# Head norms, attention and gating of a decoder trunk handed out in smaller, later pieces

## The chip, the cores and the metric

The kernel runs on one core of a Trainium2 chip. The core has a matrix engine (TensorE, PE in the profile, with its weight loads shown as PEld), a vector engine (VectorE, DVE), an engine for functions of one input (ScalarE, ACT), a general one (GpSimd, POOL) and SyncE (SP), whose queue issues most DMAs. Each engine takes the instructions of its queue in order; between engines, semaphores hold an instruction back until its inputs are written and its output's buffer is free. The metric is the device time of one execution in microseconds (us); lower is better.

## The reference

Two layers over 256 tokens of width 2048, all in float32:

```python
for l in range(DEPTH):
    h = rms_norm(x, norm1_g[l])
    z = h @ w_in[l]                                  # u | v | q | k | v of attention
    z_sgu = jax.nn.gelu(z[..., :2 * SGU_WIDTH], approximate=False)
    out_a = chunked_sgu(z_sgu, sgu_norm_g[l], sgu_w[l], sgu_b[l])
    out_b = swa_sink_attention(z[..., 2*SGU_WIDTH:q_end], z[..., q_end:k_end], z[..., k_end:], ...)
    mixed = concat([rms_norm(out_a, out_norm_a[l]), rms_norm(out_b, out_norm_b[l])])
    x = x + mixed @ w_out[l]
    h2 = rms_norm(x, norm2_g[l])
    x = x + (jax.nn.silu(h2 @ w_gate[l]) * (h2 @ w_up[l])) @ w_down[l]
```

`chunked_sgu` normalizes v per head of 64 channels, mixes it over the 128 tokens of a chunk with a lower triangular matrix, adds a bias, and multiplies u by the result. `swa_sink_attention` normalizes q and k per head, takes scores over the own block of 128 keys and the one before, adds a relative bias with a mask, and applies a softmax that has one extra "sink" logit per head; 16 query heads share 4 key heads. The feed-forward width is 5632.

## The kernel before

**Main work.** Every weight matrix is read from HBM in blocks of 256 rows by 512 columns (`raw`, 128 partitions x 1024 elements). A weight block is split into a rounded part `wh` (ScalarE, L94) and the remainder `wl` (VectorE, L95), and the activations are held as such a pair too; a product is three matmuls, high by high, high by low and low by high (L124, L125, L126). The function `unit` does this for one block and the 256 tokens: 12 matmuls of 128x128 by 512 columns. It ends with `tick()`, which moves a clock of the program by 1. There are 7 buffers for `raw`, 5 for `wh` and 4 for `wl`, so ScalarE and VectorE can work some units ahead of TensorE.

**Layer.** The projection `w_in` is taken in column blocks of 512, eight units each (`in_block`): first k and v of attention (block 6), then q (4 and 5), then v of the gating part (2 and 3), then u (0 and 1). Then follow 32 units of the output projection in eight parts (`add_part`), and the feed-forward stage, which mixes two streams of units and whose code does not change but for one short step at its start.

**Short work between.** Everything else is placed by hand between the units: `later(delay, fn)` notes a function with the program's clock plus a delay, and `tick` calls, in the order of their time and then of their noting, those that are due. A fractional time is due at the next tick that reaches it. This gives the order in which the program is written. The framework's scheduler then makes each engine's queue from it, and assigns buffers.

- `kv_norm`, `q_norm` and `v_gate` take a finished block from PSUM with ScalarE (L259, L282, L413), and norm it per head by `head_inv`: squares on ScalarE (L207), sums on VectorE (L208), then in `inv_rms` mean and epsilon on VectorE (`ms`, L169) and the power -0.5 on GpSimd (`ir`, L171). VectorE then scales by the result (L265, L287, L417, and the gain L418). All that is written in one go, right after the block. Transposes for q and k follow 4 or 5 units later.
- `attend` does one of six pieces of attention in a layer, 6, 9, 12, 15, 19 and 23 units after the first q block (`UNIT_AT`). TensorE makes the scores (`ps_s`, L319), VectorE adds the bias (`s`, L324) and takes the maximum (L333) and from it `nm` and `es` (L334, L335), ScalarE takes the exponentials with their sums (L338) and that of the sink (L342), and VectorE makes the reciprocal `rden` (L343, L344). All that is written in one go. `turn`, two units later, transposes the probabilities (`ps_p`, L352) and copies them (`pt`, L353); `weigh`, four units later, multiplies by the values (`ps_v`, L361) and scales into `ob` (L368). `attend_end` comes 6 and 7 units after the third and the sixth piece: it sums squares of `ob` (L195), transposes it (`ps_t`, L188) and splits it into the pair `aT` (L178, L179).
- `v_gate` also loads the mixing matrix `wm` and the gain `gb` from GpSimd's queue (L388, L394), masks `wm` there (L389), and 6 and 7 units later runs the mixing matmuls (`ps_g`, L404) with the bias (L410).
- `u_gated` applies Gelu (L429), multiplies by the gate (L430) and sums squares, and 2 and 3 units later transposes.
- `finish_rms` sums partial squares (L199) and calls `inv_rms` for a norm over a row; `begin` does that for the first norm of a layer, and `nr` (L530 to L532) negates the second norm's result.

**Buffers.** Small PSUM tiles come in turn from four places (`small_ps`: one of pool `pm`, two of `pd`, one of the accumulators' pool `pa`). SBUF tiles with the tag `z` share 8 places, `big` 8, `spt` 4 (scores `s` and probabilities `pt`).

Of the kernel before, what the change touches and what calls it, by code (L numbers as in the profile page):

```python
# [12 lines left out]
F32 = mybir.dt.float32  # L13
F32R = mybir.dt.float32r
BF16 = mybir.dt.bfloat16
AF = mybir.ActivationFunctionType
# [4 lines left out]
P = 128  # L21
# [42 lines left out]
def trunk(ctx, tc, x, xt, w_in, w_out, w_gate, w_up, w_down, sgu_w, sgu_g, consts,  # L64
# [135 lines left out]
        r = inv_rms(tot, NTOK, width)  # L200
        return [r[:, t : t + 1] for t in range(NTOK)]

    def head_inv(zs, n):
        ss = small([P, NTOK * n], f"hs{n}")
        for t, z in enumerate(zs):
            sq = zp.tile([P, NB], F32, tag="z", name="sq")
            nc.scalar.activation(sq[:, : n * HD], z, AF.Square)  # L207
            nc.vector.tensor_reduce(  # L208
                ss[:, t * n : (t + 1) * n],
                sq[:, : n * HD].rearrange("p (h d) -> p h d", d=HD), AX.X, ALU.add,  # L210
            )
# [28 lines left out]
    for lay in range(L):  # L240
# [14 lines left out]
        def kv_norm(acc, lay=lay, layer=layer, zkv=zkv, kT=kT):  # L255
            kd = []
            zz = ap.tile([P, NTOK, NB], F32, tag="big", name="zkv", bufs=8)
            for t in range(NTOK):
                nc.scalar.activation(zz[:, t], acc[t], AF.Copy, scale=layer["rstd1"][t])  # L259
                zkv.append(zz[:, t])  # L260
            inv = head_inv([z[:, : NKV * HD] for z in zkv], NKV)
            for t in range(NTOK):
                k = zp.tile([P, NKV, HD], F32, tag="z", name="k")
                kin = zkv[t][:, : NKV * HD].rearrange("p (h d) -> p h d", d=HD)
                nc.vector.tensor_tensor(k, kin, bc(inv[t], HD), ALU.mult)  # L265
                kd.append(k.rearrange("p h d -> p (h d)"))
# [11 lines left out]
        def q_norm(b, acc, lay=lay, layer=layer, qT=qT):  # L278
            qn = []
            for t in range(NTOK):  # L280
                z = zp.tile([P, NB], F32, tag="z", name="zq")
                nc.scalar.activation(z, acc[t], AF.Copy, scale=layer["rstd1"][t])  # L282
                qn.append(z)
            inv = head_inv(qn, 8)
            for t in range(NTOK):
                z3 = qn[t].rearrange("p (h d) -> p h d", d=HD)
                nc.vector.tensor_tensor(z3, z3, bc(inv[t], HD), ALU.mult)  # L287
# [21 lines left out]
        def attend(gp, t, i0, n, zkv=zkv, kT=kT, qT=qT, ob=ob, bias=bias, layer=layer):  # L309
# [23 lines left out]
            nc.vector.tensor_reduce(m, s, AX.X, ALU.max)  # L333
            nc.vector.scalar_tensor_tensor(nm, m, -1.0, nsink, ALU.mult, ALU.min)  # L334
            nc.vector.tensor_tensor(es, nm, nsink, ALU.subtract)  # L335
            for r in range(2):
                for i in range(n):
                    nc.scalar.activation(  # L338
                        s[:, r, i], s[:, r, i], AF.Exp, bias=nm[:, r, i : i + 1],
                        accum_out=den[:, r, i : i + 1],  # L340
                    )
            nc.scalar.activation(es, es, AF.Exp)  # L342
            nc.vector.tensor_tensor(rden, den, es, ALU.add)  # L343
            nc.vector.reciprocal(rden, rden)  # L344
            pt = ap.tile([P, 8, P], F32, tag="spt", name="pt", bufs=4)
            s8 = s.rearrange("p r i (b k) -> p (r i b) k", k=P)

            def turn():
                for half in range(2):
                    pst = small_ps([P, 4, P], "ps_p")  # L350
                    for i in range(4):
                        nc.tensor.transpose(pst[:, i, :], s8[:, 4 * half + i, :], ident)  # L352
# [32 lines left out]
        def v_gate(b, acc, lay=lay, layer=layer, gate=gate):  # L385
# [28 lines left out]
            inv = head_inv([v[:, t] for t in range(NTOK)], 8)  # L414
            for t in range(NTOK):
                v3 = v[:, t].rearrange("p (h d) -> p h d", d=HD)
                nc.vector.tensor_tensor(v3, v3, bc(inv[t], HD), ALU.mult)  # L417
                nc.vector.tensor_tensor(v[:, t], v[:, t], gb, ALU.mult)  # L418
            for half in range(2):
                later(6 + half, lambda half=half: spatial(half))  # L420

# [3 lines left out]
        def u_gated(b, acc, lay=lay, layer=layer, gate=gate, ssa=ssa, pairs_a=pairs_a):  # L425
            us = []
            for t in range(NTOK):
                u = zp.tile([P, NB], F32, tag="z", name="u")
                nc.scalar.activation(u, acc[t], AF.Gelu, scale=layer["rstd1"][t])  # L429
                nc.vector.tensor_tensor(u, u, gate[b][:, t], ALU.mult)  # L430
                sum_sq(ssa[:, t, b : b + 1], u)
                us.append(u)

            def to_T(c):
                ps = transpose_pair([us[t][:, 2 * c * P : (2 * c + 2) * P] for t in range(NTOK)])
# [31 lines left out]
        def norm_block(n, ss, pairs, lay, col, ext=None):  # L467
# [11 lines left out]
            for t in range(NTOK):  # L479
                sum_sq(ss[:, t, n : n + 1], xres[:, t, n * NB : (n + 1) * NB])  # L480

        acc_kv = in_block(6)
        if lay == 0:
            later(5, begin)
            later(5, lambda: kv_norm(acc_kv))
        else:
            begin()
            kv_norm(acc_kv)
        acc = in_block(4)
        for g in range(2):  # L490
            load_bias(g)
# [24 lines left out]
        def add_part(n, pairs, chunks, rstd):  # L516
            acc = product([w_out[lay, n, c] for c in chunks], pairs)
            for t in range(NTOK):
                xs = xres[:, t, n * NB : (n + 1) * NB]
                nc.vector.scalar_tensor_tensor(xs, acc[t], rstd[t], xs, ALU.mult, ALU.add)  # L520

        for part, n in (("b", 0), ("b", 1), ("a", 0), ("a", 1), ("b", 2), ("a", 2), ("b", 3), ("a", 3)):
            if part == "b":
                add_part(n, pairs_b, range(4, 8), rstd_b)
            else:
                add_part(n, pairs_a, range(4), rstd_a)
# [4 lines left out]
        for t in range(NTOK):  # L531
            nc.vector.tensor_scalar(nr[:, t : t + 1], rstd2[t], -1.0, None, ALU.mult)  # L532
        nrstd2 = [nr[:, t : t + 1] for t in range(NTOK)]

        ss1 = small([P, NTOK, ND], "ss4")
        pairs1 = []
# [317 lines left out]
```

## Time and profile before

| | us |
|---|---|
| three runs: median (lowest, highest) | 1946.79 (1945.83, 1951.07) |
| the profiled execution: its time | 1945.39 |
| its span, first to last instruction | 1943.6 |
| TensorE busy | 1927.1 |
| VectorE busy | 1659.8 |
| ScalarE busy | 1301.4 |
| GpSimd busy | 122.0 |

The granted clock of TensorE was 1.00 throughout. A row of the page or of a view names an engine, a line of the kernel, an operation, what it writes and reads, and the shapes; then busy time and, in brackets, the idle time of the engine just before and what ended it. "PE ps_p L352 <- ACT s L338" reads: TensorE, about to write `ps_p` in line 352, waited for ScalarE writing `s` in line 338. Rows of a timeline start with the time and the duration in us. Busy spans of matmuls are modelled and overlap, so two consecutive ones count for less than their sum. Layer 0 reaches the feed-forward stage at about 300 us, layer 1 begins at about 975 us and reaches its own at about 1265 us.

### The profile page before, as it was taken

To read this page: it belongs to the slowest core of one execution; us is meant where nothing else is said; L and a number is where in the kernel's file an instruction comes from. 1 tells how busy PE (TensorE), PEld (TensorE's weight loads), DVE (VectorE), ACT (ScalarE), POOL (GpSimd) and SP (SyncE) were. 2 spreads that over 40 slices of the span, in tenths; PEclk is the share of its full clock that TensorE was granted. 3 is DMA by queue.
4 is the path that set the end of the run, shared out by engine and by line. 5 is a ranking of instruction groups with operands and counts; after the bars stand their busy time and mean duration, and the time that the engine had idled before them with its cause. 6 is when DMAs were issued, how large, how long until landed. Compare 5 with 4: busy or idle time off the path is not lost.

```text
span 1943.6 us, 25049 instructions
## 1 busy us (share of the span) xinstructions
PE 1927.1 (99%) x8836; PEld 1576.2 (81%) x8836; DVE 1659.8 (85%) x1752; ACT 1301.4 (67%) x1729; POOL 122.0 (6%) x124
## 2 busy tenths in 40 slices
PE   9999999999999999999999999999999999999999
PEld 6788887878888888888887888878788888888887
DVE  6566689999999999999556656899999999999993
ACT  7565566667767776777756755666677767767675
POOL 1210000000000000000002000000000000000000
PEclk9999999999999999999999999999999999999999
DMA  9544557667867786778555345586678676776783
GB/s 364 194 144 154 186 174 230 219 230 242 260 216 236 241 275 210 240 228 271 195 198 191 132 164 183 169 260 213 212 241 280 211 242 225 269 218 236 238 264 125
DMA packets 118958, 426.41 MB, mean 219 GB/s; under 512 B 13232, under 2 KB 13872, under 8 KB 118832
## 3 DMA queue, kind: packets, MB, share of 16 engines
q1 hardware_dynamic: 105264, 375.52, 52.7%
q0 software_dynamic: 13568, 49.29, 13.7%
q8 instruction: 69, 1.13, 0.2%
q14 instruction: 57, 0.47, 0.1%
HBM read 422.66 MB, written 2.10 MB: 219 GB/s over the span
## 4 chain that ended last, share of the span: by engine, by line
PE 92%; issue 3%; DVE 2%; ACT 1%; POOL 1%; DMA 1%; SPq 0%; ACTq 0%; DVEq 0%; POOLq 0%
PE m L125 13%; PE m L124 13%; PE m L126 13%; PE acc L125 8%; PE acc L126 8%; PE acc L124 8%; PE dacc L125 8%; PE dacc L124 8%; PE dacc L126 8%; PE ps_f L188 1%; POOL ir L171 1%; PE ps_v L361 1%; DVE wl L95 1%; PE ps_n L188 1%; ACT s L338 0%
## 5 line engine op out<-in xcount | busy, mean ns | idle before, releaser
L94 ACT CAST wh<-raw 128x1024 fp32r<-128x1024 f32 (+1 forms) x786 | 803.8, 1049 | 451.5 <-DVE raw L591 167.3
L95 DVE TENSOR_TENSOR wl<-raw,wh 128x1024 fp32r<-128x1024 f32 (+1 forms) x786 | 934.4, 1216 | 160.3 <-PE acc L125 90.7
L124 PE MATMUL m<-wh,ext 128*128 128x512 f32 x640 | 252.0, 395 | 0.7 <-ACT wh L94 0.7
L125 PE MATMUL m<-wl,ext 128*128 128x512 f32 x640 | 251.7, 393 | 0.7 <-DVE wl L95 0.6
L126 PE MATMUL m<-wh,ext 128*128 128x512 f32 x640 | 250.2, 391 | 0.0
L124 PE MATMUL dacc<-wh,aT 128*128 128x512 f32 x576 | 224.6, 391 | 0.9 <-ACT wh L94 0.9
L125 PE MATMUL dacc<-wl,aT 128*128 128x512 f32 x576 | 224.4, 390 | 0.1
L126 PE MATMUL dacc<-wh,aT 128*128 128x512 f32 x576 | 224.3, 389 | 0.0
L95 DVE TENSOR_TENSOR wl<-t,wh 128x1024 fp32r<-128x1024 f32 x160 | 193.7, 1218 | 3.5 <-issue 1.7
L94 ACT CAST wh<-t 128x1024 fp32r<-128x1024 f32 x160 | 168.1, 1052 | 38.3 <-DVE t L592 12.5
L125 PE MATMUL m<-wl,hT 128*128 128x512 f32 x480 | 187.2, 390 | 0.0
L126 PE MATMUL m<-wh,hT 128*128 128x512 f32 x480 | 186.8, 389 | 0.0
L124 PE MATMUL m<-wh,hT 128*128 128x512 f32 x480 | 186.5, 389 | 0.0
L124 PE MATMUL acc<-wh,hT 128*128 128x512 f32 x448 | 179.5, 403 | 1.0 <-ACT wh L94 1.0
L125 PE MATMUL acc<-wl,hT 128*128 128x512 f32 x448 | 176.1, 393 | 1.1 <-DVE wl L95 1.1
L126 PE MATMUL acc<-wh,hT 128*128 128x512 f32 x448 | 175.8, 392 | 0.0
L597 POOL DMA_DIRECT2D t<-in_w_gate_dram x80 | 68.4, 855 | 1326.3 <-DVE wl L95 1122.0
L124 PE MATMUL acc<-wh,aT 128*128 128x512 f32 x384 | 151.6, 395 | 0.0
L126 PE MATMUL acc<-wh,aT 128*128 128x512 f32 x384 | 150.0, 391 | 0.0
L125 PE MATMUL acc<-wl,aT 128*128 128x512 f32 x384 | 149.6, 389 | 0.0
L125 PEld LDWEIGHTS m<-wl,ext 128*128 128x128 f32 x640 | 120.2, 188 | 32.4 <-DVE wl L95 8.5
L124 PEld LDWEIGHTS m<-wh,ext 128*128 128x128 f32 x640 | 120.1, 188 | 27.2 <-ACT wh L94 2.6
(138 smaller groups left out, 2704.9 us busy)
## 6 DMA issues: line engine op xcount, KB each, us to landing
raw<-in_w_gate_dram SPq DMA_DIRECT2D x176, 512.0 KB, 5.6
raw<-in_w_up_dram SPq DMA_DIRECT2D x176, 512.0 KB, 5.6
raw<-in_w_down_dram SPq DMA_DIRECT2D x176, 512.0 KB, 4.8
raw<-in_w_in_dram SPq DMA_DIRECT2D x108, 512.0 KB, 4.3
t<-in_w_gate_dram POOLq DMA_DIRECT2D x80, 512.0 KB, 5.7
raw<-in_w_out_dram SPq DMA_DIRECT2D x64, 512.0 KB, 3.3
bias<-in_band_dram POOLq DMA_DIRECT2D x8, 512.0 KB, 4.4
xr<-in_xt_dram SPq DMA_DIRECT2D x8, 256.0 KB, 5.9
```

The costliest lines, as they stand in the source:

```text
L94: nc.scalar.copy(wh[:, j : j + step, :], src)
L95: nc.vector.tensor_tensor(wl[:, j : j + step, :], src, f(wh[:, j : j + step, :]), ALU.subtract)
L124: nc.tensor.matmul(acc, ah, wh, start=first, stop=False, skip_group_check=again)
L125: nc.tensor.matmul(acc, ah, wl, start=False, stop=False, skip_group_check=again)
L126: nc.tensor.matmul(acc, al, wh, start=False, stop=last, skip_group_check=again)
L171: anchor[0] = nc.gpsimd.tensor_tensor(r, ms, mhalf[:, :n], ALU.pow)
L188: nc.tensor.transpose(ps[:, j, t * P : (t + 1) * P], blocks[t][:, j * P : (j + 1) * P], ident)
L361: nc.tensor.matmul(pv[:, r, i], pt[:, (r * n + i) * (t + 1) + b, :], zkv[b][:, cols], start=b == 0, stop=b == t,)
L597: nc.gpsimd.dma_start(t2, w_gate[lay, b, i, 1], accum_op=ALU.add)
```

## The change

The pieces of short work that wait for another engine are cut where they wait, and each part is noted for a later tick:

- `head_inv` no longer returns the result. It writes the squares at once, the sums, mean and power one unit later, and hands the scaling, as a function, to 1.5 units after that.
- In `attend` the exponentials are written one unit after the scores, `turn` three units after (two before), `weigh` five (four before). `rden` is made in `weigh`, and the tile `pt` is taken in `turn`.
- In `u_gated` the multiplication comes one unit later and the sums of squares two units later.
- In layer 1, `begin` is written after the first unit of the kv block (after its eighth before), and `kv_norm` one unit after the block's end. In layer 0 `begin` comes one unit sooner than before.
- The row norms of the two mixed parts are written three units into the output projection, and the negation two units into the feed-forward stage.
- The instruction behind which `wm` is queued (`layer["anchor"]`, the last power written so far) becomes an earlier one, since the power of the first q block is now written after that line.

```diff
-    def head_inv(zs, n):
-        ss = small([P, NTOK * n], f"hs{n}")
-        for t, z in enumerate(zs):
+    def head_inv(zs, n, then):
+        sqs = []
+        for z in zs:
             sq = zp.tile([P, NB], F32, tag="z", name="sq")
             nc.scalar.activation(sq[:, : n * HD], z, AF.Square)
-            nc.vector.tensor_reduce(...)
-        r = inv_rms(ss, NTOK * n, HD)
-        return [r[:, t * n : (t + 1) * n] for t in range(NTOK)]
+            sqs.append(sq)
+
+        def power():
+            ss = small([P, NTOK * n], f"hs{n}")
+            for t, sq in enumerate(sqs):
+                nc.vector.tensor_reduce(...)
+            r = inv_rms(ss, NTOK * n, HD)
+            later(1.5, lambda: then([r[:, t * n : (t + 1) * n] for t in range(NTOK)]))
+
+        later(1, power)
...
-            inv = head_inv(qn, 8)
-            for t in range(NTOK):
-                z3 = qn[t].rearrange("p (h d) -> p h d", d=HD)
-                nc.vector.tensor_tensor(z3, z3, bc(inv[t], HD), ALU.mult)
+            def scaled(inv):
+                for t in range(NTOK):
+                    z3 = qn[t].rearrange("p (h d) -> p h d", d=HD)
+                    nc.vector.tensor_tensor(z3, z3, bc(inv[t], HD), ALU.mult)
+
+            head_inv(qn, 8, scaled)          # kv_norm and v_gate in the same way
...
-            for r in range(2):
-                for i in range(n):
-                    nc.scalar.activation(s[:, r, i], ..., AF.Exp, ...)
-            nc.scalar.activation(es, es, AF.Exp)
-            nc.vector.tensor_tensor(rden, den, es, ALU.add)
-            nc.vector.reciprocal(rden, rden)
-            pt = ap.tile([P, 8, P], F32, tag="spt", name="pt", bufs=4)
+            def exps():
+                for r in range(2):
+                    for i in range(n):
+                        nc.scalar.activation(s[:, r, i], ..., AF.Exp, ...)
+                nc.scalar.activation(es, es, AF.Exp)
...
             def turn():
+                pt = ap.tile([P, 8, P], F32, tag="spt", name="pt", bufs=4)
+                pts.append(pt)
...
             def weigh():
+                pt = pts[0]
+                nc.vector.tensor_tensor(rden, den, es, ALU.add)
+                nc.vector.reciprocal(rden, rden)
...
-            later(2, turn)
-            later(4, weigh)
+            later(1, exps)
+            later(3, turn)
+            later(5, weigh)
...
-                nc.vector.tensor_tensor(u, u, gate[b][:, t], ALU.mult)
-                sum_sq(ssa[:, t, b : b + 1], u)
                 us.append(u)
...
+            later(1, gated)
+            later(2, squares)
...
+        if lay > 0:
+            later(1, begin)
         acc_kv = in_block(6)
         if lay == 0:
-            later(5, begin)
+            later(4, begin)
             later(5, lambda: kv_norm(acc_kv))
         else:
-            begin()
-            kv_norm(acc_kv)
+            later(1, lambda: kv_norm(acc_kv))
...
-        rstd_b = finish_rms(ssb, SW)
-        rstd_a = finish_rms(ssa, SW)
+        later(3, finish_mixed)               # both, into rstds["b"] and rstds["a"]
...
-        for t in range(NTOK):
-            nc.vector.tensor_scalar(nr[:, t : t + 1], rstd2[t], -1.0, None, ALU.mult)
+        later(2, negate)                     # the same
```

More of the change, by code (lines that the diff above doesn't have):

```diff
@@ L260, in kv_norm @@
                 zkv.append(zz[:, t])
-            inv = head_inv([z[:, : NKV * HD] for z in zkv], NKV)
-            for t in range(NTOK):
[L263 to L266, printed above, removed]
+            def scaled(inv):
+                for t in range(NTOK):
+                    k = zp.tile([P, NKV, HD], F32, tag="z", name="k")
+                    kin = zkv[t][:, : NKV * HD].rearrange("p (h d) -> p h d", d=HD)
+                    nc.vector.tensor_tensor(k, kin, bc(inv[t], HD), ALU.mult)
+                    kd.append(k.rearrange("p h d -> p (h d)"))
+            head_inv([z[:, : NKV * HD] for z in zkv], NKV, scaled)
             def to_T():
@@ L413, in v_gate, with scaled @@
                 nc.scalar.activation(v[:, t], acc[t], AF.Gelu, scale=layer["rstd1"][t])
[L414 to L418, printed above, removed]
+            def scaled(inv):
+                for t in range(NTOK):
+                    v3 = v[:, t].rearrange("p (h d) -> p h d", d=HD)
+                    nc.vector.tensor_tensor(v3, v3, bc(inv[t], HD), ALU.mult)
+                    nc.vector.tensor_tensor(v[:, t], v[:, t], gb, ALU.mult)
+            head_inv([v[:, t] for t in range(NTOK)], 8, scaled)
             for half in range(2):
@@ L519, in add_part @@
                 xs = xres[:, t, n * NB : (n + 1) * NB]
[L520 removed]
+                nc.vector.scalar_tensor_tensor(
+                    xs, acc[t], rstds[kind][t], xs, ALU.mult, ALU.add
+                )
         for part, n in (("b", 0), ("b", 1), ("a", 0), ("a", 1), ("b", 2), ("a", 2), ("b", 3), ("a", 3)):
             if part == "b":
[L524 removed]
+                add_part(n, pairs_b, range(4, 8), part)
             else:
[L526 removed]
+                add_part(n, pairs_a, range(4), part)
                 norm_block(n, ss2, pairs2, lay, C_G2, ext2)
```

35 lines of the change are left out of this document (25 added, 10 removed).

## The prediction

> **What bounds the kernel now.** I read the page first: its span, its busy line and its chain.
>
> ```profile
> span 1943.6 us, 25049 instructions
> ...
> PE 1927.1 (99%) x8836; PEld 1576.2 (81%) x8836; DVE 1659.8 (85%) x1752; ACT 1301.4 (67%) x1729; POOL 122.0 (6%) x124
> ...
> PE 92%; issue 3%; DVE 2%; ACT 1%; POOL 1%; DMA 1%; SPq 0%; ACTq 0%; DVEq 0%; POOLq 0%
> ```
>
> TensorE is busy for 1927.1 of 1943.6 us and holds 92% of the chain that ended last. It can stand idle for 16.5 us in all, so no change that leaves its instructions alone, as this one does, can win more than that. The profiled execution took 1945.39 us, 1.79 us beyond its span; the median of the three runs, 1946.79, is 1.40 us above it. The sum is made on 1945.39 and those 1.40 us are added at the end.
>
> Second, the windows: how much of that idle time lies where the change works. That is the projections, the attention and the output projection of each layer, 60 to 320 us and 960 to 1290 us. The first columns are the window's length and the busy time of TensorE.
>
> ```profile
> 60.00:320.00 260.00, 256.24 (x1281) 210.76 (x1280) 182.73 (x255) 158.67 (x273) 20.71 (x17) 1.00 0.51 172
> 960.00:1290.00 330.00, 327.88 (x1604) 268.17 (x1603) 224.56 (x306) 204.14 (x342) 28.03 (x22) 1.00 0.53 176
> 80.00:100.00 20.00, 17.70 (x98) 13.74 (x97) 14.76 (x24) 11.02 (x22) 6.59 (x5) 1.00 0.52 173
> 120.00:140.00 20.00, 18.55 (x104) 15.10 (x103) 15.60 (x27) 14.81 (x30) 3.50 (x2) 1.00 0.31 99
> 1040.00:1060.00 20.00, 18.89 (x99) 14.63 (x98) 11.87 (x20) 13.61 (x39) 5.08 (x4) 1.00 0.26 88
> 1080.00:1100.00 20.00, 19.05 (x111) 15.61 (x111) 10.98 (x22) 17.80 (x41) 3.50 (x2) 1.00 0.12 40
> 180.00:200.00 20.00, 20.00 (x93) 16.54 (x93) 11.04 (x13) 10.59 (x15) 0.00 (x0) 1.00 0.54 183
> ```
>
> The idle time is 3.76 us in layer 0 and 2.12 us in layer 1, 5.88 together. Four windows of 20 us hold nearly all of it: 2.30, 1.45, 1.11 and 0.95, together 5.81 us. The last row is an undisturbed window: 93 matrix instructions in 20.00 us, 0.215 each, so that a unit of main work (12 of them) is about 2.6 us. The remaining 10.6 us of idle time are the first loads and the feed-forward stages, which the change does not touch.
>
> Third, the waits: who waits for whom (total us, times, longest).
>
> ```profile
> DVE hs L208 <- ACT sq L207: 13.6, 9, 3.5
> DVE v L417 <- POOL ir L171: 12.3, 4, 3.1
> DVE zq L287 <- POOL ir L171: 10.9, 4, 2.8
> DVE rden L343 <- ACT es L342: 10.4, 6, 2.5
> ...
> PE ps_p L352 <- ACT s L338: 3.2, 2, 2.3
> PE ps_v L361 <- DVE aT L179: 1.8, 2, 0.9
> PE acc L125 <- DVE wl L95: 1.1, 3, 0.6
> ```
>
> VectorE heads its queue with another engine's short step for 13.6 + 12.3 + 10.9 + 10.4 = 47.2 us. That is the change's target, but only 5.6 of it (2.3 + 0.9 + 0.6 in layer 0, 0.9 + 0.9 in layer 1) reaches TensorE; the other 41.6 us lie under the main work. So the ceiling is under 6 us, 0.30%, of what looks like 47.
>
> **Part by part.** Every edit re-dates work; none adds or drops an instruction, and no matmul changes. So each term is a stall that goes, stays or appears.
>
> *The stall at 89 us (q1 norm, unit 1 of attention).* The timeline, VectorE then TensorE:
>
> ```profile
> 77.78 0.17 DVE L343 TENSOR_TENSOR rden<-den,es 128x8 f32<-128x8 f32 x1 [2.03 <-ACT es L342]
> 80.40 1.28 DVE L208 TENSOR_REDUCE hs<-sq 128x8 f32<-128x512 f32 x2 [2.22 <-ACT sq L207]
> 81.86 1.23 DVE L95 TENSOR_TENSOR wl<-raw,wh 128x1024 fp32r<-128x1024 f32 x1
> 85.92 1.29 DVE L287 TENSOR_TENSOR zq<-zq,ir 128x512 f32<-128x512 f32 x2 [2.83 <-POOL ir L171]
> 87.13 1.28 DVE L324 SCALAR_TENSOR_TENSOR s<-ps_s,bias 128x512 f32<-128x512 f32 x2
> 92.03 0.44 PE L352 MATMUL ps_p<-ident,s 128*128 128x128 f32 x2 [2.30 <-ACT s L338]
> ```
>
> Three waits in a row (the sink's exponential, the squares, the power; 2.03 + 2.22 + 2.83 us) put the scores s, and with them the maximum and the exponentials, behind them, and the transposes ps_p, which need the exponentials, wait 2.30 us. The change moves the sink sum and reciprocal to the weighing, five units after the scores, the reduction one unit and the scaling three ticks after the squares (1 + 1.5, run at a whole tick), behind the scores of that unit, and the transposes one unit later. Without the scaling's wait of 2.83 us and its work of 1.29 the scores come 4.1 us sooner, and the transposes ask 2.6 us later: a margin of 6.7 against a stall of 2.3. I take the whole 2.30.
>
> *The same in layer 1, and its staircase.*
>
> ```profile
> 1054.03 1.29 DVE L287 TENSOR_TENSOR zq<-zq,ir 128x512 f32<-128x512 f32 x2 [2.46 <-POOL ir L171]
> 1057.81 1.91 PE L352 MATMUL ps_p<-ident,s 128*128 128x128 f32 x8 [0.94 <-ACT s L338]
> ...
> 1071.89 0.87 PE ps_p L352 x8
> ```
>
> The scaling, waiting, stands again ahead of the exponentials that ps_p waits for. I take the whole idle time of that window, 1.11. The eight transposes took 1.91 us here and 0.87 a little later in the same layer (the last row, from the chain): up to 1.04 us more of crawling behind single exponentials, which the windows count as busy; I take none of it and give it to a rival.
>
> *The stalls at 129 and 1095 us (v norm beside the end of the first attention half).*
>
> ```profile
> 108.82 1.05 ACT L94 CAST wh<-raw 128x1024 fp32r<-128x1024 f32 x1 [1.62 <-issue]
> 125.05 1.99 ACT L94 CAST wh<-raw 128x1024 fp32r<-128x1024 f32 x2
> ...
> 124.51 1.29 DVE L417 TENSOR_TENSOR v<-v,ir 128x512 f32<-128x512 f32 x2 [3.04 <-POOL ir L171]
> 132.21 1.22 DVE L95 TENSOR_TENSOR wl<-raw,wh 128x1024 fp32r<-128x1024 f32 x1
> ...
> 129.52 1.97 PE L361 MATMUL ps_v<-zkv,pt 128*128 128x64 f32 x16 [0.87 <-DVE aT L179]
> 133.48 0.50 PE L125 MATMUL acc<-wl,hT 128*128 128x512 f32 x1 [0.58 <-DVE wl L95]
> ```
>
> ScalarE rounded no weight from 108.82 + 1.05 to 125.05, 15.2 us or about six units: it ran Gelu, exponentials, squares and copies, all written ahead of the next weight. VectorE's next wl began at 132.21, and TensorE waited first for a PSUM tile (ps_v, freed by aT) and then for that wl. The change spreads what lay in one unit (attend_end, scores and weigh, four small PSUM tiles with four places) over two, which should free ps_v. But ScalarE's work at this place stays as large, and the wl behind it stays late: with the weigh a unit later, TensorE comes to the missing wl with 1.97 us less to do. Between nothing (the stall moves from ps_v to wl) and all of 1.45 + 0.95 = 2.40, I take half, 1.20.
>
> *Waits the change adds.* Weigh moves to 5 units after the scores, attend_end stays at 6: its transposes of ob, at the head of TensorE's queue, now have one unit (2.6 us) instead of two after ps_v. What VectorE must do between is the multiply into ob; the wait for es (longest 2.5 us above) that can stand ahead of it moves too, so I take nothing; if ob is queued behind a power wait of 3.04 the stall is 3.04 + 1.29 - 2.6 = 1.7 us in each layer, 3.4 in all. Reverse side: none, no transposes of ob wait for anything today. Kv norm one unit later in layer 1, gating one, its squares and the final norms two and three units later, and the negation two units into the feed-forward stage: their consumers come at least a unit after, under main work that no wait interrupts now (180 to 200 us: 20.00 of 20.00 busy); nothing, and if that cover goes, one power wait each, 1 to 3 us. Begin in layer 1 is written seven units sooner, for the same instant:
>
> ```profile
> 976.92 0.72 POOL L171 TENSOR_TENSOR ir<-ms,mhalf 128x2 f32<-128x2 f32 x1 [72.16 <-DVE ms L169]
> ```
>
> Today it is written after the eight kv units, of which nearly all were still to come at 976.92 (a unit is 2.6 us, and the stage before ended in the 960 window): the order in a queue isn't the order written, work that is ready is pulled ahead. The anchor of the wm loads becomes an earlier power, so wm may go sooner; none of TensorE's 5.6 us is for it.
>
> [...] The change wants wl to run on VectorE while GpSimd computes the power.
>
> ```profile
> 81.98 3.90 POOL L171 TENSOR_TENSOR ir<-ms,mhalf 128x16 f32<-128x16 f32 x1 [21.41 <-DVE ms L169]
> 1051.07 2.93 POOL L171 TENSOR_TENSOR ir<-ms,mhalf 128x16 f32<-128x16 f32 x1 [22.68 <-DVE ms L169]
> 1058.13 1.09 POOL L389 TENSOR_SCALAR_AFFINE_SELECT wm<-wm 128x1024 f32<-128x1024 f32 x1 [3.59 <-DMA wm<-in_sgu_w_dram]
> ...
> 1058.17 1.06 DVE L335 TENSOR_TENSOR es<-nm,nsink 128x4 f32<-128x4 f32 x1
> 293.67 0.71 POOL L171 TENSOR_TENSOR ir<-ms,mhalf 128x2 f32<-128x2 f32 x1 [0.27 <-DVE ms L169]
> 293.94 1.23 DVE L95 TENSOR_TENSOR wl<-raw,wh 128x1024 fp32r<-128x1024 f32 x1 [0.36 <-PE dacc L125]
> ```
>
> A power that met the wl of 81.86 took 3.90, one that met none 2.93: 0.97 us more for GpSimd. The other way, the small es that began inside the affine select took 1.06, as long as the select; but the wl of 293.94, begun inside a power, ran its usual 1.23. So a power lengthens by up to 0.97 beside wl and doesn't hold wl up. The power is off the path with three ticks allowed: nothing in the sum. [...]
>
> **The sum.** 1945.39 - 2.30 - 1.11 - 1.20 = 1940.78 on the profiled execution; with the 1.40, 1942.2 us, 0.24% less. With none or all of the 2.40: 1943.4 to 1941.0.
>
> **The rivals.** *All stalls go* (0.22): 5.81 us and the 1.04 of the crawling transposes, 6.85 us: 1939.9 us, 0.35% less. For it: every one of these waits starts with a step that the change re-dates. Against: ScalarE's 15.2 us.
>
> *It does not do what it says* (0.12): the row of 976.92 shows ready work pulled ahead of its place. A later place only lowers precedence, and the scaling may still head VectorE's queue: 0 to 1.2 us won, 1946.
>
> *GpSimd's queue blocked on a buffer* (0.22), which ends slower. The pool z has 8 places. The two squares of a norm now both stay until the reduction a unit later, beside kT, two ob, two gb and the void of a sum. If none is free, the load of gb waits at the head of GpSimd's queue, and v's power behind it.
>
> ```profile
> 97.78 0.53 POOL L388 DMA_DIRECT2D wm<-in_sgu_w_dram  x1 [6.36 <-DVE s L324]
> ```
>
> That load waited 6.36 us for a place in another pool; the same ahead of v's power would come on top of the 3.04 where TensorE's lead is used up: 6.36 us a layer, less the 3.41 won: 1949.7 in one layer, 1956.1 in both. It decides only if gb comes ahead of the power with all eight places held; today the power does not wait so.
>
> **How the numbers follow.** The forecast has 0.44. A measurement of this kernel tells some 0.3% from no change, 5.84 us: 1940.95 and 1952.63. Forecast (0.44), no effect (0.12) and the blocked queue in one layer (0.07) are the same: 0.63; all stalls gone 0.22 faster; blocked in both 0.15 slower. The forecast's own range is 1941.0 to 1943.4. The range runs from 1938, two us below the faster case (the fastest run before lies 0.96 below its median), to 1953, past the one-layer block and the 3.4 us of the ob wait; it leaves out the block in both layers.
>
> **What would show it.** Right: the 80 and 1040 windows full, s L324 no longer behind zq's wait, rden's and hs's waits nearly gone, one or two short waits for wl near 129 and 1095, feed-forward stages as long as now. Wrong: waits of ps_t for ob near 120 and 1088, GpSimd waiting at gb (L394), more table loads on ScalarE, or the same chain at 89 us.

## The result, and the profile after

| us | before | after |
|---|---|---|
| six runs each, on the same chip: median (lowest, highest) | 1946.64 (1945.64, 1951.07) | 1940.54 (1939.52, 1941.01) |
| the profiled execution | 1945.39 | 1940.95 |

The ratio is 0.9966, with a 95% interval of 0.9956 to 0.9976: 6.1 us or 0.34% less, against a forecast of 1942.2 us and a range of 1938 to 1953. The page of the changed kernel, the lines that answer to those shown of before:

```profile
span 1939.2 us, 25050 instructions
...
PE 1925.2 (99%) x8836; PEld 1578.4 (81%) x8836; DVE 1660.9 (86%) x1752; ACT 1301.4 (67%) x1729; POOL 123.2 (6%) x124
...
PE 94%; issue 2%; DVE 2%; ACT 1%; POOL 0%; DMA 0%; SPq 0%; ACTq 0%; DVEq 0%; POOLq 0%
```

Every engine has as many instructions as before, and TensorE's share of the chain rose from 92 to 94%. The windows of the changed kernel show where. After the stretch and its length stand busy time and instructions of TensorE, its weight loads, VectorE, ScalarE and GpSimd, and behind the brackets TensorE's granted clock, the share of the DMA engines and GB/s:

```profile
60.00:320.00 260.00, 259.98 (x1300) 215.04 (x1299) 187.61 (x258) 159.63 (x273) 21.49 (x15) 1.00 0.54 175
80.00:100.00 20.00, 20.00 (x115) 16.47 (x113) 15.36 (x26) 13.62 (x31) 8.45 (x5) 1.00 0.65 210
120.00:140.00 20.00, 20.00 (x115) 16.50 (x114) 17.15 (x29) 14.80 (x25) 0.00 (x0) 1.00 0.56 178
955.00:1285.00 330.00, 326.78 (x1602) 268.97 (x1602) 224.56 (x306) 204.25 (x342) 28.37 (x22) 0.99 0.54 176
1075.00:1095.00 20.00, 18.93 (x111) 16.02 (x110) 12.54 (x24) 16.25 (x38) 3.50 (x2) 1.00 0.28 91
1059.80:1063.20 3.40, 3.40 (x9) 2.63 (x9) 0.93 (x3) 2.32 (x10) 0.00 (x0) 0.50 0.86 274
```

In layer 0 TensorE is idle for 0.02 us where it was for 3.76. In layer 1 (the window lies 5 us sooner, as the layer does) it is idle for 3.22 us where it was for 2.12, and for 3.4 us its granted clock is 0.50: in that window it is busy throughout and starts 9 matrix instructions where full speed has 15 (3.4 us at 0.227 us each, the median distance of consecutive starts of the main work in this trace). So in this execution one layer won all, and the other won nothing. The same by starts, from the first matmul of a layer's unit 9 (layer 0) or unit 1 (layer 1) to the first of its feed-forward stage:

| us | before | after |
|---|---|---|
| layer 0 | 30.84 to 289.83: 258.99 | 30.16 to 284.82: 254.66 |
| feed-forward of layer 0 | 289.83 to 973.99: 684.16 | 284.82 to 969.19: 684.37 |
| layer 1 | 973.99 to 1257.09: 283.10 | 969.19 to 1252.60: 283.41 |

Layer 0 gives 4.33 us and layer 1 takes 0.31. Layer 1 has the 3.4 us at half clock in that, which cost about 1.4 us (six matrix instructions of 0.227 fewer) and are not in every execution: in three of the six runs the mean granted clock was 1.000. The waits of the changed kernel (total us, times, longest), VectorE's first, then TensorE's:

```profile
DVE v L439 <- POOL ir L171: 12.3, 4, 3.1
...
DVE zq L298 <- POOL ir L171: 9.9, 4, 2.8
DVE rden L374 <- ACT es L357: 9.3, 6, 2.0
DVE hs L213 <- ACT sq L207: 9.3, 9, 2.1
...
PE ps_p L369 <- DVE s L337: 2.1, 1, 2.1
PE ps_s L332 <- DVE aT L179: 1.1, 1, 1.1
```

The four sums that were 47.2 us are 40.8. The queue is still headed by waits for short steps nearly as long as before, and yet layer 0 has no stall left. What changed is seen in the timeline of VectorE, around the place where TensorE stood for 2.30 us, with TensorE's next scores and transposes behind it:

```profile
81.36 1.28 DVE L337 SCALAR_TENSOR_TENSOR s<-ps_s,bias 128x512 f32<-128x512 f32 x2
84.28 0.69 DVE L298 TENSOR_TENSOR zq<-zq,ir 128x512 f32<-128x512 f32 x1 [1.63 <-POOL ir L171]
...
91.40 1.13 PE L332 MATMUL ps_s<-kT,qT 64*128 64x256 f32 x8
92.57 1.29 DVE L337 SCALAR_TENSOR_TENSOR s<-ps_s,bias 128x512 f32<-128x512 f32 x2
92.96 1.04 PE L369 MATMUL ps_p<-ident,s 128*128 128x128 f32 x8
```

The scores s now run at 81.36, ahead of the scaling's wait; before, they ran at 87.13, behind it. The wait for the power is still there, but only work with time to spare is behind it. The two stalls of layer 1 are new ones. The timeline of the changed kernel at both places, with GpSimd (POOL) and VectorE beside TensorE:

```profile
1054.39 1.13 PE L332 MATMUL ps_s<-kT,qT 64*128 64x256 f32 x8
1054.66 2.22 POOL L410 TENSOR_SCALAR_AFFINE_SELECT wm<-wm 128x1024 f32<-128x1024 f32 x1 [3.67 <-DMA wm<-in_sgu_w_dram]
1054.70 1.22 DVE L95 TENSOR_TENSOR wl<-raw,wh 128x1024 fp32r<-128x1024 f32 x1
...
1055.93 2.03 DVE L95 TENSOR_TENSOR wl<-raw,wh 128x1024 fp32r<-128x1024 f32 x1
1055.95 0.60 PE L369 MATMUL ps_p<-ident,s 128*128 128x128 f32 x4
...
1057.88 1.27 DVE L337 SCALAR_TENSOR_TENSOR s<-ps_s,bias 128x512 f32<-128x512 f32 x2
1058.70 0.63 PE L369 MATMUL ps_p<-ident,s 128*128 128x128 f32 x4 [2.15 <-DVE s L337]
...
1086.37 0.69 DVE L439 TENSOR_TENSOR v<-v,ir 128x512 f32<-128x512 f32 x1 [3.11 <-POOL ir L171]
1086.97 0.48 DVE L179 SCALAR_TENSOR_TENSOR aT<-ps_t,cst,aT 128x256 fp32r<-128x256 f32 x1
1089.19 1.13 PE L332 MATMUL ps_s<-kT,qT 64*128 64x256 f32 x8 [1.07 <-DVE aT L179]
```

At 1058.70 the second half of a turn waits for s, which does not write what it reads but frees a place: two tiles of scores, one for the transposes of q and two of ps_p are asked for in one unit, five small PSUM tiles, and there are four places. With `turn` two units after the scores they fell in different units; with three they meet the scores of the next piece. The same five tiles meet in layer 0 (scores at 91.40, both halves of the turn at 92.96) without a wait: there VectorE runs s 1.2 us after the scores began, at 92.57, and here 3.5 us after, at 1057.88, behind two wl. So it takes both, the missing place and a VectorE that comes late. At 1089.19 the scores wait for aT, which frees their place and stands on VectorE behind the scaling of v, which waits 3.11 us for its power.

### The profile page after: what moved, and what is told of

It reads as the page before. It is cut to its first block, busy times and chain, and to the rows that moved or that the text cites. A ratio compares the mean times of both kernels' runs of the same rounds, so it can differ in the third digit from the quotient of the medians.

```text
span 1939.2 us, 25050 instructions
## 1 busy us (share of the span) xinstructions
PE 1925.2 (99%) x8836; PEld 1578.4 (81%) x8836; DVE 1660.9 (86%) x1752; ACT 1301.4 (67%) x1729; POOL 123.2 (6%) x124
## 4 chain that ended last, share of the span: by engine, by line
PE 94%; issue 2%; DVE 2%; ACT 1%; POOL 0%; DMA 0%; SPq 0%; ACTq 0%; DVEq 0%; POOLq 0%
PE m L125 13%; PE m L124 13%; PE m L126 13%; PE acc L124 9%; PE acc L126 9%; PE acc L125 9%; PE dacc L125 8%; PE dacc L124 8%; PE dacc L126 8%; PE ps_f L188 1%; DVE wl L95 1%; PE ps_v L381 1%; PE ps_n L188 1%; PE ps_s L332 1%; PE ps_t L188 0%
```

## The experiments

Each was run beside the kernel before on its chip, whose median there was 1946.28 to 1947.18 us. One table for those with a ratio: median us, ratio to before with its 95% interval, then from the profiled execution the stretches of layers 0 and 1 as defined above and the time at half clock in the whole main work, by the trace's record of the granted clock.

| | median | ratio | layer 0 | layer 1 | half clock |
|---|---|---|---|---|---|
| before | 1946.64 | 1 | 258.99 | 283.10 | 0 |
| after | 1940.54 | 0.9966 (0.9956 to 0.9976) | 254.66 | 283.41 | 3.4 |
| e1_head | 1942.16 | 0.9976 (0.9965 to 0.9987) | 256.88 | 281.31 | 0 |
| e2_attn | 1942.31 | 0.9973 (0.9962 to 0.9983) | 254.29 | 285.67 | 10.2 |
| e3_rest | 1946.97 | 1.0000 (0.9990 to 1.0009) | 260.57 | 283.23 | 10.2 |
| e4_turn | 1943.00 | 0.9977 (0.9968 to 0.9986) | 258.01 | 282.84 | 6.8 |
| e9_dist | 1943.08 | 0.9979 (0.9970 to 0.9988) | 254.29 | 285.76 | 10.2 |
| e5_q1 | 1938.24 | 0.9958 (0.9945 to 0.9972) | 254.67 | 279.42 | 3.4 |
| e6_v | 1939.34 | 0.9965 (0.9953 to 0.9977) | 254.29 | 282.20 | 3.4 |
| e7_both | 1936.33 | 0.9948 (0.9936 to 0.9961) | 254.33 | 278.30 | 0 |
| e10_pow2 | 1944.75 | 0.9989 (0.9980 to 0.9998) | 258.60 | 282.79 | 3.4 |
| e11_pow2_before | 1967.92 | 1.0109 (1.0092 to 1.0125) | 268.44 | 292.44 | 20.5 |

### Which part of the change does it

Three kernels take one part each of the change, on before. e1_head takes `head_inv` in pieces, with its three callers:

```diff
-        r = inv_rms(ss, NTOK * n, HD)            # with the sums, in one go
...
+            r = inv_rms(ss, NTOK * n, HD)        # with the sums, in power
+            later(1.5, lambda: then([r[:, t * n : (t + 1) * n] for t in range(NTOK)]))
...
+        later(1, power)
```

> The kernel before with the head norms of k, q and v cut in two later pieces, nothing else changed. Theory 1 (order: the scaling that waited for the power no longer stands ahead of the scores on VectorE): the scores of the second attention piece come some 3 us sooner, the wait of 2.30 us at 89 us and the one of 0.94 at 1058 us go or fall under 0.5; the waits of ps_v at 129 and 1096 us stay (0.9 each); 2.5 to 3.5 us faster than before. Theory 2 (distance: what helps is that the transposes of the probabilities ask one unit, 2.6 us, later): the stall at 89 us stays at 1.5 us or more, under 1 us faster.

e2_attn takes the body of `attend`:

```diff
+            later(1, exps)                 # rden in weigh, pt taken in turn
-            later(2, turn)
-            later(4, weigh)
+            later(3, turn)
+            later(5, weigh)
```

> The kernel before with attention alone cut: exponentials one unit after the scores, transposes three, weighing five, the reciprocal with the weighing. Theory 1 (order): the scaling still stands ahead of the scores and waits 2.8 us for the power; the stall at 89 us shrinks by the 2.6 us that the transposes come later, so it goes, but the next weight remainder comes late; 2 to 3 us faster. Theory 2 (distance): all of layer 0's gain, 4 to 4.5 us faster, and both of layer 1's new stalls (2.15 us before the second half of the transposes, 1.07 us before scores) appear here as well.

e3_rest takes the remainder: gating, the dates of `begin` and `kv_norm`, the mixed norms, the negation:

```diff
+            later(1, gated)
+            later(2, squares)
...
-            begin()
-            kv_norm(acc_kv)
+            later(1, lambda: kv_norm(acc_kv))      # later(1, begin) ahead of the block
...
+        later(3, finish_mixed)
+        later(2, negate)
```

> The kernel before with the remaining edits alone: gating one unit later and its squares two, the first norm of layer 1, kv norm, the norms of the mixed parts and the negation re-dated. Both theories: nothing that TensorE waits for is touched; within 0.7 us of before, the same four stalls.

TensorE's waits in the layers, first of e1_head:

```profile
PE ps_v L374 <- DVE aT L179: 2.1, 2, 1.1
```

TensorE's waits of e2_attn:

```profile
PE ps_s L319 <- DVE aT L179: 1.8, 1, 1.8
...
PE ps_p L356 <- DVE s L324: 1.3, 1, 1.3
```

TensorE's waits of e3_rest:

```profile
PE ps_p L352 <- ACT s L338: 3.2, 2, 2.3
PE ps_v L361 <- DVE aT L179: 1.9, 2, 1.1
```

e3_rest has before's waits to within 0.2 us, and its ratio is 1, with an interval of 0.1% on either side: the gating, the row norms and the negation do nothing that can be measured. e1_head loses both waits for ps_p, at 89 and 1057 us, and keeps those for ps_v (2.1 us): it wins 2.1 us in layer 0 and 1.8 in layer 1. e2_attn loses all of these, wins 4.7 us in layer 0, and brings both new ones of layer 1, where it is 2.6 us slower than before, with 6.8 us at half clock. So either part removes the stalls for ps_p, only the attention part those for ps_v, and only the attention part makes the new stalls.

### Order or distance in the attention

e4_turn is after with the old two numbers; e9_dist is before with the new two numbers and nothing else, so that the exponentials and `rden` stay where they were.

```diff
# e4_turn, on after                     # e9_dist, on before
-            later(3, turn)             -            later(2, turn)
-            later(5, weigh)            -            later(4, weigh)
+            later(2, turn)             +            later(3, turn)
+            later(4, weigh)            +            later(5, weigh)
```

> The changed kernel with transposes and weighing back at two and four units after the scores (exponentials stay at one, the reciprocal stays in the weighing). Theory 1 (order): layer 0 as in the changed kernel within 1 us; in layer 1 the new wait of 2.15 us at 1057 us goes, since scores, q transposes and probability transposes no longer ask for five small PSUM tiles in one unit with four places; about the changed kernel's time or up to 2 us less. Theory 2 (distance): the stall at 89 us comes back with 1.5 us or more, and that of ps_v at 129 us; 2 to 4 us slower than the changed kernel.

> The kernel before with two numbers changed: the transposes of the probabilities three units after the scores and the weighing five, instead of two and four; exponentials and reciprocal are written with the scores as before, and no other edit is made. Theory 1 (distance between a step and its consumer on TensorE): the waits at 89 us and at 129 us go as in the run of attention alone, layer 0 is 4 to 5 us shorter, layer 1 shows the same two new waits of 1.3 to 2.2 us; the time of the run of attention alone (1942.3) within 1 us. Theory 2 (the later exponentials and the later reciprocal matter, since they leave VectorE and ScalarE free for the next weights): layer 0 gains under 3 us, and a wait for es of over 2 us stands ahead of the scores.

TensorE's waits of e4_turn:

```profile
PE ps_v L381 <- DVE aT L179: 2.1, 2, 1.1
```

TensorE's waits of e9_dist:

```profile
PE ps_s L319 <- DVE aT L179: 1.8, 1, 1.8
...
PE ps_p L352 <- DVE s L324: 1.3, 1, 1.3
```

e4_turn has e1_head's waits (its stretches are 1.1 and 1.5 us longer, with 3.4 us at half clock in each layer). e9_dist has those of e2_attn, and its two stretches agree with e2_attn's within 0.1 us. Their ratios differ by less than their intervals. Hence the cutting of `attend` into pieces does nothing here that can be measured: of that part of the change, the two numbers are all that the time shows.

### The two new stalls, taken away

If the stall at 1058 us is five tiles for four places, it goes when the transposes of the second q block come a unit later (e5_q1). If the one at 1089 is aT behind the waiting scaling of v, it goes when that scaling is put behind the aT in VectorE's queue (e6_v). e7_both has both edits.

```diff
# e5_q1
-                later(4 + c, lambda c=c: to_T(c))
+                later(4 + b + c, lambda c=c: to_T(c))
# e6_v: split_last is the last VectorE instruction of split_gain (aT, L179)
-                for t in range(NTOK):            # in v_gate's scaled
+                with tc.issue_after(split_last[0].ins):
+                    for t in range(NTOK):
...
```

> The changed kernel with the transposes of the second q block one unit later (13 and 14 units after the first block instead of 12 and 13). Theory 1 (places: in the unit 12 after the first q block the change has five small PSUM tiles asked for, two of scores, one of q, two of probabilities, where there are four places): the wait of 2.15 us at 1057 us in layer 1 goes, layer 0 stays as it is, the wait of 1.07 us at 1088 us stays; 1.5 to 2.5 us faster than the changed kernel's 1940.54, more if the half clock that followed the stall goes too. Theory 2 (VectorE's queue: three remainders wl, one of them held up beside GpSimd's mask, stand ahead of the scores' add): the wait stays at 1.5 us or more; within 0.7 us of the changed kernel.

> The changed kernel with the scaling of the gating's v queued on VectorE behind the last split of attention's output (aT) that was written, instead of ahead of it. Theory 1 (the wait that the change meant to remove is still there: v's scaling waits 3.11 us for the power at the head of VectorE's queue, holds aT back, and so the PSUM place that the next scores need): the wait of 1.07 us of ps_s for aT at 1088 us goes, and VectorE's waits of v for ir fall from 12.3 us by 2 to 5; 0.7 to 1.5 us faster than the changed kernel. Theory 2 (VectorE simply has too much to do there): the wait turns into one for a weight remainder of the same length; within 0.5 us.

> Both edits in one kernel. Theory 1 (two stalls, each its own cause): no wait over 0.5 us on TensorE in either layer's attention; 1936.5 to 1938, 2.5 to 4 us faster than the changed kernel. If the gains are one stall moved about: 1939 or more.

The one wait above 1 us that TensorE has left in the layers of e5_q1, in its view of waits:

```profile
PE ps_s L332 <- DVE aT L179: 1.1, 1, 1.1
```

The same of e6_v, and VectorE's waits for the power of v, in its view of waits:

```profile
PE ps_p L370 <- DVE s L338: 2.1, 1, 2.1
...
DVE v L441 <- POOL ir L172: 6.2, 2, 3.1
```

The timeline of e6_v's VectorE at the second place:

```profile
1084.37 0.48 DVE L180 SCALAR_TENSOR_TENSOR aT<-ps_t,cst,aT 128x256 fp32r<-128x256 f32 x1 [1.33 <-ACT aT L179]
...
1086.84 1.28 DVE L441 TENSOR_TENSOR v<-v,ir 128x512 f32<-128x512 f32 x2
```

Each edit takes its own stall and leaves the other. The traces tell this; by time neither kernel can be told from after, since all three intervals overlap. In e6_v the aT runs 2.5 us ahead of the scaling of v, and two of the four waits for v's power are gone. The windows of e7_both:

```profile
60.00:320.00 260.00, 259.99 (x1301) 215.05 (x1300) 188.20 (x259) 160.00 (x274) 22.82 (x17) 1.00 0.54 174
950.00:1280.00 330.00, 329.99 (x1624) 272.12 (x1624) 225.66 (x307) 208.46 (x351) 28.90 (x22) 1.00 0.54 179
```

TensorE is idle for 0.02 us in both stretches together. e7_both takes 1936.33 us (1935.33 to 1936.61), 10.0 us less than before's 1946.28 on its chip. After, on another chip, was 6.1 us below before there, so the two edits are worth 3.9 us by these differences and 3.5 by the ratios; none of e7_both's runs comes within 2.9 us of any of after's. Layer 1 is 5.11 us shorter than in after; the two stalls are 3.22 of that, and the 3.4 us at half clock, gone as well, cost about 1.4 (six matmuls of 0.227 us fewer, as shown above).

### What the mask on GpSimd adds

At 1055.93 a wl took 2.03 us where others take 1.22, beside the affine select of GpSimd. The wl ahead of it, begun at 1054.70 just after the select, took its usual 1.22, and the select 2.22. e8_nomask is after without it, so that the mixing matrix is not masked; one execution, 1939.08 us. If the select has part in the stall of 2.15 us, the second wl takes its usual 1.22 here and the stall is some 0.8 us shorter; if it has none, the stall stays.

```diff
-            nc.gpsimd.affine_select(out=wm, in_=wm, ...)
```

> The changed kernel without the triangular mask on the mixing matrix wm (the affine select on GpSimd is left out; the rest is the same). [...]

Its timeline, at the place of the first new stall:

```profile
1056.57 1.20 DVE L95 TENSOR_TENSOR wl<-raw,wh 128x1024 fp32r<-128x1024 f32 x1
...
1058.52 0.63 PE L369 MATMUL ps_p<-ident,s 128*128 128x128 f32 x4 [1.31 <-DVE s L337]
```

The wl takes 1.20 and the stall 1.31 instead of 2.15. Some 0.8 us of the stall are the select; the other 1.3 go only with the missing place, as in e5_q1.

### How much delay each queue forgives

If the queue of the changed kernel has slack, then a longer power should cost it less. In both kernels a second power of the same size is put ahead of each power of the q and v norms (16 columns), on e7_both (e10_pow2) and on before (e11_pow2_before): eight more powers in the two layers, by estimate of about 2.9 us each (2.93 at 1051.07 in before), 23 us of GpSimd.

```diff
+        if n == 2 * NTOK * NKV:
+            twice = small([P, n], "twice")
+            nc.gpsimd.tensor_tensor(twice, ms, mhalf[:, :n], ALU.pow)
         anchor[0] = nc.gpsimd.tensor_tensor(r, ms, mhalf[:, :n], ALU.pow)
```

> The kernel with both edits (1936.33), with each of the eight powers of q and v done twice on GpSimd, the first into a tile that nobody reads: some 2.9 us more between the mean and the scaling, 23 us in all. Theory 1 (a wait at the head of VectorE's queue costs nothing as long as the next main work and the next consumer on TensorE have their lead): VectorE's waits for ir grow by 10 to 23 us, TensorE's waits by less than 2, the time by less than 2. Theory 2 (what waits on VectorE reaches TensorE sooner or later): 6 us or more.

> The kernel before with the same eight powers done twice. Theory 1: the scaling stands ahead of what TensorE waits for in four of the eight places (89, 129, 1057, 1095 us), so up to 2.9 us more in each: 6 to 12 us slower than before, and several times what the same doubling costs the kernel with both edits. Theory 2: about the same cost in both kernels.

The waits of TensorE and VectorE in e10_pow2:

```profile
PE acc L125 <- DVE wl L95: 3.7, 4, 1.6
PE ps_p L373 <- DVE rden L378: 1.6, 1, 1.6
...
DVE zq L302 <- POOL ir L175: 21.4, 4, 5.7
...
DVE v L444 <- POOL ir L175: 16.7, 4, 6.0
```

The same of e11_pow2_before:

```profile
PE ps_p L355 <- ACT s L341: 9.0, 2, 5.2
PE ps_v L364 <- DVE aT L182: 7.6, 2, 3.8
...
DVE v L420 <- POOL ir L174: 23.9, 4, 6.0
DVE zq L290 <- POOL ir L174: 22.4, 4, 5.7
```

Both pay: e10_pow2 8.4 us (1944.75 - 1936.33; 7.5 when each is set against before on its own chip), e11_pow2_before 20.7 us (1967.92 - 1947.18, before's median on that chip). I expected next to nothing for e10_pow2, and that was wrong: a wait of 5.7 us for a power still heads VectorE's queue there, and TensorE then waits for wl and, at the transposes, for VectorE. In before the same wait stands ahead of what TensorE asks for next: the four stalls are 5.17, 3.77, 3.83 and 3.83 us, where they were 2.30, 0.87, 0.94 and 0.95. Each has grown by 2.87 to 2.90 us, the length of one power (e11's timeline: 2.90). So these four stalls hang on the power with no slack at all. The four together are 11.5 us more; with six times 3.4 us at half clock, about 1.4 each, that makes 19.9, where the profiled executions lie 19.2 apart. The changed kernel forgives about 60% of the extra delay (8.4, or 7.5, against 20.7), not all.

## Why the prediction was right, and where it was not

*The outcome.* 1940.54 lies 1.7 us below the forecast and 0.5 below the lower end of its own range (1941.0). It is 0.34% less where 0.3% was taken as what can be told from no change, so the result falls narrowly to "faster", which had 0.22, and not to "same", which had 0.63; the interval of the ratio (0.24 to 0.44%) lies on both sides of that line.

*The sum.* On the profiled execution it came within 0.2 us: 1940.78 was worked out and 1940.95 measured. That is luck. Layer 0 gave 4.33 us where 2.30 and half of 1.45 were taken (3.0); layer 1 lost 0.31 where 1.11 and half of 0.95 were to be won (1.6); and layer 0's unit 9 began 0.68 us sooner, which no term had and which varies from kernel to kernel (30.10 to 31.46 us). The 1.7 us between forecast and median come from the 1.40 that was added at the end: after's median lies 0.41 below its profiled execution, not 1.40 above it.

*The stall at 89 us, 2.30, taken whole.* Right, with its reason: the scores ran at 81.36 instead of 87.13, 5.8 us sooner, of which 0.7 is the sooner start (4.1 was the estimate), and the turn found its exponentials. e1_head alone and e9_dist alone remove it as well, so the margin of 6.7 us was made of two parts of which each is enough.

*Layer 1's 1.11 us, taken whole.* The old wait went and a longer one came: 2.15 us. The step that failed is taking the old stall as the whole term: I asked only whether the exponentials would come sooner, and not what the moved transposes would meet. The four places for small PSUM tiles stand in the prediction at 129 us, but I did not count them in the unit where turn, scores and transposes of q meet. That is the term with the wrong sign, and in the profiled execution 3.4 us at half clock followed it.

*Half of 2.40 for 129 and 1095 us.* The value came near by a sum of two halves that were each off. In layer 0 the whole 1.45 went, in layer 1 the 0.95 came back as 1.07 at 1089 us. The fear behind the half did not come true: ScalarE still rounds no weight for 11.9 us (105.6 to 117.5, 15.2 before), and does as much in the window 120 to 140 as before (14.80 us, 14.81), but the waits for wl near 129 and 1095, which the prediction named as a sign, did not come.

*The ceiling of 5.88 us.* Wrong: e7_both, with the same matrix instructions, wins 4.66 in layer 0 and 4.80 in layer 1, 9.5 us. A matmul's modelled duration is 0.39 us where the next starts 0.227 after it, so each stall looks 0.16 us shorter than it is, and TensorE that follows a slow engine looks busy. Of the latter kind were the transposes of 1.91 us at 1057, which I gave to a rival; in e7_both they took 1.09. Idle time (5.88), 0.16 for each of five stalls and that 0.82 make 7.5; the other 2.0 stay open. By count of instructions the window view comes nearer: layer 0's 260 us hold 1281 in before and 1300 in after, and 19 times the 0.215 of the prediction's own row are 4.1 us, where the starts show 4.33 and the idle time fell by 3.74.

*Nothing for re-dated gating, row norms, negation, begin.* Right as far as can be told: e3_rest has the ratio 1.0000 (0.9990 to 1.0009).

*Waits added.* The wait of ob behind the weighing took nothing, as assumed; the changed kernel has no wait of ps_t for ob. The blocked queue of GpSimd did not occur: VectorE's waits for v's power are 12.3 us in both. *It does not do what it says* was half true: the waits for powers, squares and exponentials hardly fell (47.2 to 40.8), though rden's and hs's were to be nearly gone (9.3 us each, from 10.4 and 13.6). What it did is put the scores ahead of the waiting scaling and TensorE's askings later.

*VectorE beside GpSimd, nothing in the sum.* For the powers nothing speaks against it: the four wl of after that begin inside one (33.61, 288.93, 972.54 and 1256.71 us; powers of 0.7 us) took 1.23. The affine select is another matter: 2.22 us at 1054.66 where another took 1.09 (1065.05), and of the two wl begun inside it the second took 2.03 instead of 1.22. The first, begun 0.04 us behind the select by the profile's start times, took its usual 1.22. Without the select (e8_nomask) the second takes 1.20. By what mechanism the two hold each other up, no run here shows.

## What to carry to other kernels

What a wait at the head of a queue costs depends on what stands behind it. Most of the 47.2 us of such waits reached no stall of TensorE, but at four places each added us cost TensorE a us. Look at which work the next consumer asks for, and put that ahead of the wait. When a step is moved by one unit, count every shared buffer place in the unit where it lands; here a fifth tile for four places brought a stall of 2.15 us. And where ends are modelled, count instructions per window or distances of starts, not idle time, to know what can be won.

## What was not expected of the hardware

A stall costs more than its length in some executions. After the stall of 2.15 us in after, the granted clock fell to 0.50 from 1059.8 to 1063.2. In e3_rest a stall of exactly the length of before's was followed by the same, and in before it was not; the timeline of e3_rest:

```profile
92.27 0.44 PE L352 MATMUL ps_p<-ident,s 128*128 128x128 f32 x2 [2.30 <-ACT s L338]
92.47 0.48 PE L125 MATMUL acc<-wl,hT 128*128 128x512 f32 x1
...
93.25 0.77 PE L124 MATMUL acc<-wh,hT 128*128 128x512 f32 x1
...
95.53 0.63 PE L124 MATMUL acc<-wh,hT 128*128 128x512 f32 x1
```

The clock fell at 93.0: the matmul of the main work ahead of it lasts 0.48 us, those behind it 0.63 to 0.77. Layer 0 lasted 1.58 us longer than before's with the same waits. In e11_pow2_before, with stalls of 3.8 to 5.2 us, all four were followed by half clock; of stalls of 1 to 2.3 us some were and others not (e4_turn's of 1.04 at 127 us was, e1_head's of 1.04 at the same place wasn't), and e5_q1 had it at 414.5 in the feed-forward stage, where TensorE's longest wait was 0.45 us, but three waits in the 3.4 us ahead made 1.20 and it started 8 instructions where 15 have room. All these times are 3.4 or 6.8 us long. Their price shows best in the feed-forward stage of layer 0, whose main work is the same in all kernels: it lasted 685.5 to 686.0 us in the four that had one there (e2_attn, e3_rest, e5_q1, e9_dist) and 684.1 to 684.7 in the others, about 1.4 us less.

The time at half clock in after lasted 3.413 us by the record, and within a trace the changes of the clock lie whole multiples of that, more closely 3.4133, apart: in after the clock fell at 1059.80 and, near the end, at 1937.02 us, 257 times; in e11_pow2_before at 94.48, 135.44, 1070.69 and 1111.65 us, 12, 274 and 12 times. Both pairs of equal stalls differ in where they lie on this grid. The two that were followed by half clock lay whole in one stretch of it (89.97 to 92.27 in 89.63 to 93.05 for e3_rest, 126.00 to 127.04 in 125.80 to 129.21 for e4_turn), and the two that weren't were cut by an edge (before's at 90.24, 543 times 3.4133 ahead of its only fall, at 1943.68 behind the last instruction; e1_head's at 125.73). That does not tell all of them apart: e1_head's 1.11 us up to 1091.40 lay whole in 1088.29 to 1091.70 and were not followed by it.

Stalls well under 3.4 us were enough: e4_turn's lasted 1.04. What makes the clock fall, and why on this grid, no run here shows.

The course of the clock is known of profiled executions alone, but its mean is on record for every run, and the time goes with it: e2_attn took 1940.2 and 1940.5 us at a mean of 1.000 and 1944.0 and 1944.3 at 0.997, and before, in its 56 runs beside the experiments, 1945.6 on average at 1.000, 1946.7 at 0.999 and 1948.3 at 0.998. So such times make much of a kernel's spread. They do not make the change's gain: after took 1939.9 on average at 1.000 (three runs) and 1940.8 at 0.999 (three), 5.7 and 5.9 us less than before at the same means.
